# A decoder layer's recurrence: triangular products with a head's 64 columns as weights, two heads side by side, and turned back

## The chip, the cores and the metric

The kernel runs on one core of one Trainium2 chip. The metric is the device time of one execution in microseconds (us). Three executions of the kernel before took 2217.72 to 2218.32 us, median 2218.01 us.

## The reference, cut to what matters

The kernel computes one decoder layer on 256 tokens of width 2048, in float32: a SwiGLU feed-forward block, a mixer (sliding-window attention beside an RWKV-7 recurrence), cross-attention into a fixed memory, a second feed-forward block and a final norm. The parts that the change touches are the recurrence and the scores of the cross-attention:

```python
def rwkv7_scan(r, w, k, v, a, b):          # 16 heads of 64
    def step(S, inp):
        r_t, w_t, k_t, v_t, a_t, b_t = inp
        sa = jnp.einsum('bhij,bhj->bhi', S, a_t)
        S = S * w_t[:, :, None, :] + sa[..., None] * b_t[:, :, None, :] + v_t[..., None] * k_t[:, :, None, :]
        return S, jnp.einsum('bhij,bhj->bhi', S, r_t)
...
    s = jnp.einsum('bthd,bmhd->bhtm', q, km).astype(jnp.float32) * (CROSS_HEAD_DIM ** -0.5)
```

## The kernel before, in words

Precision first. A float32 product of the large matrices is done as three products of a faster format ("fp32r"): each operand is split into a high part, rounded by a ScalarE copy (line 345), and a low part, the rest, by a VectorE subtraction (line 346). Lines 438 to 440 multiply high by high, high by low and low by high into the same bank of PSUM. These are the main matrix products; their weights stream in through the SP queue in items of 1 MB or less. The recurrence and the cross-attention's scores use plain fp32 matmuls, which the profile records twice each.

The order of the work is written out by hand as an interleaving. Each background step is a Python generator; `bg.tick()` lets the first steps of each group (`const`, `feat`, `attn`, `ew`, `inverse`, `chain`, `norm`, `mem`) advance by one `yield`, and a tick comes after each six main matmuls or so. `yield from idle(n)` waits n ticks. A scheduler then orders each engine's queue: among instructions that its model finds ready, the one written first goes first. So a step's place in the trace is not its place in the file, and a `yield` moves a priority more than a time. `issue_after` adds an order on an engine's own queue.

The recurrence is solved in two chunks (c = 0, 1) of 128 tokens for two halves (h = 0, 1) of eight heads each. In `chain(h)` a half goes through these steps. `masked(c, m)` makes, per head, a 128 by 128 product of keys and receptances and masks it to a triangle (`mk`). `known(c)` multiplies `mk[c, 0]` by the values and, for c = 1, adds the state `s0` times the removal keys; the result is `u`. `solved(c)` multiplies the inverse of a triangle (`xb`) by `u`, giving `sa`. `results(c)` adds up three products into the output `yq`. Between the chunks the state `s0` is formed. `known` (line 1453) and `solved` (line 1470) use the triangle as the weights, 128 rows by 128 columns, and a head's 64 columns as the moving operand. `results` (line 1488) has it the other way round already: a head's 64 columns are the weights, the triangle moves, and the two heads of a pair write PSUM partitions 0 to 63 and 64 to 127 in turn. `invert(h)` builds `xb`, `finish(h)` normalises `yq` and leaves `yr`, the input of the products with `w_proj_rwkv`.

SBUF tiles come from pools with few buffers: `half` (five, for `u`, `sa`, `s0` and the like) and `t4` (20 of 4 KB per partition, for nearly all else in the mixer). PSUM has four single banks (`acc`) and two pairs (`two`); `acc` is shared by main products and chain steps.

Other places that the change touches: `late_vectors` (line 264) loads three small tables on the POOL queue; `to_features` (line 913) turns a product's tokens into features, one ScalarE copy out of PSUM; `attend` (line 924) is the windowed attention with its softmax on VectorE and ScalarE; `decay_and_rate` (line 1084), `substitute` (line 1235) and `invert` (line 1327) run ahead of the chain; `look_up` (line 1684) is the cross-attention, whose scores are fp32 matmuls at line 1693.

Of the kernel before, what the change touches and what calls it, by code (L numbers as in the profile page):

```python
# [142 lines left out]
def decoder_layer(ctx: ExitStack, tc: tile.TileContext, a: dict, out: bass.AP):  # L143
# [120 lines left out]
    def late_vectors():  # L264
        yield from idle(60)
        pool.dma_start(gains[:], a["g_later"])
        pool.dma_start(rv[:], a["v_rwkv"])
        pool.dma_start(sinks[:], a["attn_sinks"].broadcast_to([P, 16]))
        yield from idle(20)
        dve.tensor_scalar(nk_k[:], k_k, -1.0, None, ALU.mult)  # L270
        dve.tensor_scalar(ok_a[:], k_a, -1.0, 1.0, ALU.mult, ALU.add)
# [620 lines left out]
    with tc.tile_pool(name="mx", bufs=1, reuse_waits="tile") as sp:  # L892
# [20 lines left out]
        def to_features(tok, dst, name):  # L913
            last = act.copy(dst[:], feats(tok))
# [9 lines left out]
        def attend(kvs, qb):  # L924
# [32 lines left out]

            m, nm, es, den = (each(name) for name in ("m", "nm", "es", "den"))
            b3 = b[:].rearrange("p e (c w) -> p (e c) w", w=w)
            s3 = s[:].rearrange("p e c w -> p (e c) w")  # L960
# [21 lines left out]
            )  # L982
            yield from idle(5 if nk == 2 and kvs[0] else 4)
            pt = t4("pt", (P, 2, 4, P))
# [99 lines left out]
        def decay_and_rate():  # L1084
# [8 lines left out]
            for h in range(2):  # L1093
                cs.append(t4("cs"))
                aa.append(t4("aa"))
                for q in (0, 2):
                    b = two()
                    by_turns(
                        (
                            b[:, e, i * T : (i + 1) * T],  # L1100
                            wa[64 * e : 64 * e + 64, (4 * h + q + i) * P : (4 * h + q + i + 1) * P],
                            xwa[64 * e : 64 * e + 64, :],
                        )
                        for i in range(2) for e in (1, 0)
                    )
                    for i in range(2):
                        for e, (dst, bias) in enumerate(((cs[h], w0), (aa[h], a0))):
                            c = 4 * h + q + i
                            rates = act.activation(
                                dst[:, q + i, :], b[:, e, i * T : (i + 1) * T], AF.Sigmoid,  # L1110
                                bias=bias[:, c : c + 1],
                            )
                yield from idle(4)
            for h in range(2):
# [120 lines left out]
        def substitute():  # L1235
# [18 lines left out]
            pool.dma_start(xd[:].rearrange("i h u t -> (i h) u t"), xt[:])  # L1254
            act.copy(tmp[:96], xt[:96].rearrange("p u t -> p t u"))
            pool.dma_start(xe[:].rearrange("i h t u -> (i h) t u"), tmp[:96])
# [70 lines left out]
        def invert(h):  # L1327
# [60 lines left out]
            act.copy(n2_[low].rearrange("p c n t -> p c (n t)"), b[low])  # L1388
            yield
            b = two()  # L1390
# [19 lines left out]
        def chain(h):  # L1410
# [5 lines left out]
            ah, bh, kh, rh = at_[h], bt[h], aa[h], rt[h]  # L1416
            mk, u, sa = {}, {}, {}

# [16 lines left out]
            def masked(c, m):  # L1435
# [11 lines left out]
                )  # L1447

            def known(c):
                b = acc()  # L1450
                for j in range(4):
                    for e in range(2):
                        pe.matmul(  # L1453
                            b[:, of(j, e)], mk[c, 0][:, e, j, :], vtok[h][:, c, of(j, e)],
                            start=j + e == 0, stop=c == 0, **ek,
                        )
                if c:
                    for j in range(4):
                        pe.matmul(
                            b[:, at(j)], ah[:, j, at(c)], s0[:, at(j)], start=False, stop=True,  # L1460
                            **ek,
                        )
                u[c] = wide("u")
                act.copy(u[c][:], b)

            def solved(c):
                b = acc()
                for j in range(4):
                    for e in range(2):
                        pe.matmul(  # L1470
                            b[:, of(j, e)], xb[h][c][:, 4 * e + j, :], u[c][:, of(j, e)],
                            start=j + e == 0, stop=True, **ek,
                        )
                sa[c] = wide("sa")
                act.copy(sa[c][:], b)

# [31 lines left out]
            masked(0, 2)  # L1508
            yield
            solved(0)  # L1510
            bk = turned()
            masked(1, 0)
            yield
            results(0)
# [12 lines left out]
            masked(1, 2)  # L1527
            yield
            solved(1)
            yield  # L1530
            results(1)
# [142 lines left out]

        km, vm, qc = t4("km"), t4("vm", (P, 2, 512)), t4("qc")
        bg.until(lambda: hasattr(nm_, "r"))
# [7 lines left out]
        def look_up(t):  # L1684
# [7 lines left out]
            for h in range(4):  # L1692
                pe.matmul(b4[:, h], qc[:, h, ts], km[:, h, :], start=True, stop=True)
            dve.tensor_reduce(m[:], b4, AX.X, ALU.max)
# [160 lines left out]
```

## Time and profile before

| what | value |
|---|---|
| median of three executions | 2218.01 us |
| the profiled execution, its own time | 2218.37 us |
| its span, first to last instruction | 2216.6 us |
| TensorE (PE) busy | 2202.8 us |
| VectorE (DVE) busy | 1761.8 us |
| ScalarE (ACT) busy | 1197.5 us |

The profile has one row per instruction. PE is the matmul, PEld the weight load that runs beside it. A row `acc<-vtok,mk 128*128 128x64` is a matmul into a bank `acc`, from the tiles `vtok` and `mk`, with weights of 128 rows by 128 columns and a moving operand of 128 partitions by 64 columns. The view called the chain follows the work that ended last back to the start; there each row gives a start in us and the time by which the piece moved the end on, and xN is the number of records. A row of the timeline gives a start, a duration and, in brackets, the engine's idle time just before it and what ended that. Matmuls overlap, so a matmul's duration there is longer than its share of the engine's time.

### The profile page before, as it was taken

What the parts mean: (1) busy time and instruction counts of PE and PEld (TensorE: products, weight loads), DVE (VectorE), ACT (ScalarE), POOL (GpSimd) and SP (SyncE); (2) the same over time, 40 slices, a digit from 0 to 9 for tenths busy, and PEclk for the clock granted to TensorE, in tenths of its full rate; (3) what the DMA queues carried; (4) which work ended last, traced back from release to release, by engine and by line L of the source; (5) the groups of instructions that cost most, each with busy time, mean ns of one, the idle gap of its engine ahead of it and who ended that gap; (6) DMA issues with size and microseconds to landing.
All of it is one profiled execution on the core that took longest, in us unless ns stands there. A gap on an engine that the chain in (4) does not pass through costs nothing.

```text
span 2216.6 us, 28327 instructions
## 1 busy us (share of the span) xinstructions
PE 2202.8 (99%) x10774; PEld 1816.7 (82%) x10774; DVE 1761.8 (79%) x2053; ACT 1197.5 (54%) x1447; POOL 72.2 (3%) x141
## 2 busy tenths in 40 slices
PE   9999999999999999999999999999999999999998
PEld 7888888888888877888888888888888888888886
DVE  8988988898887477888556676558888988898887
ACT  6555555555555557534445455556555555555554
POOL 1000000000000000010400000000000000000000
PEclk9999999999999999999999999999999999999999
DMA  7665665565656545677714765557565565565564
GB/s 261 205 219 194 204 207 192 190 209 190 209 178 220 171 128 155 214 230 222 206 54 150 235 218 202 184 171 262 193 206 185 196 209 191 188 209 196 203 207 153
DMA packets 220536, 433.31 MB, mean 195 GB/s; under 512 B 13952, under 2 KB 16336, under 8 KB 220400
## 3 DMA queue, kind: packets, MB, share of 16 engines
q1 hardware_dynamic: 213200, 410.70, 56.0%
q0 software_dynamic: 6624, 20.14, 2.9%
q8 instruction: 84, 1.38, 0.2%
q10 hardware_dynamic: 576, 0.66, 0.1%
q14 instruction: 52, 0.43, 0.1%
HBM read 419.00 MB, written 12.45 MB: 195 GB/s over the span
## 4 chain that ended last, share of the span: by engine, by line
PE 96%; DVE 1%; DMA 1%; ACT 1%; issue 1%; SPq 0%; POOLq 0%; POOL 0%; ACTq 0%; DVEq 0%
PE acc L438 21%; PE acc L439 21%; PE acc L440 21%; PE two L438 9%; PE two L439 9%; PE two L440 9%; PE two L187 2%; PE two L179 1%; DMA raw<-in_ffn_w_up_dram 1%; DVE lo L346 1%; PE two L1351 0%; PE acc L1488 0%; PE acc L1453 0%; PE acc L1470 0%; PE acc L1351 0%
## 5 line engine op out<-in xcount | busy, mean ns | idle before, releaser
L345 ACT CAST hi<-raw 128x1024 fp32r<-128x1024 f32 (+1 forms) x769 | 762.8, 1001 | 791.8 <-PE two L440 370.5
L346 DVE TENSOR_TENSOR lo<-raw,hi 128x1024 fp32r<-128x1024 f32 (+1 forms) x770 | 884.3, 1158 | 321.2 <-ACT hi L345 320.0
L438 PE MATMUL acc<-hi,xhi 128*128 128x512 f32 (+1 forms) x1224 | 478.1, 391 | 1.2 <-ACT hi L345 0.8
L439 PE MATMUL acc<-lo,xhi 128*128 128x512 f32 (+1 forms) x1224 | 475.2, 388 | 1.3 <-DVE lo L346 1.3
L440 PE MATMUL acc<-hi,xlo 128*128 128x512 f32 (+1 forms) x1224 | 474.3, 388 | 0.0
L438 PEld LDWEIGHTS acc<-hi,xhi 128*128 128x128 f32 x1224 | 229.7, 188 | 52.9 <-issue 3.9
L439 PEld LDWEIGHTS acc<-lo,xhi 128*128 128x128 f32 x1224 | 230.0, 188 | 49.5 <-DVE lo L346 3.7
L440 PEld LDWEIGHTS acc<-hi,xlo 128*128 128x128 f32 x1224 | 229.9, 188 | 46.4 <-DVE xlo L712 0.2
L371 DVE TENSOR_TENSOR tlo<-raw,thi 128x1024 fp32r<-128x1024 f32 x160 | 193.1, 1221 | 0.0
L370 ACT CAST thi<-raw 128x1024 fp32r<-128x1024 f32 x160 | 165.7, 1050 | 33.3 <-DVE raw L365 18.8
L439 PE MATMUL acc<-lo,hhi 128*128 128x512 f32 x424 | 166.5, 393 | 0.0
L440 PE MATMUL acc<-hi,hlo 128*128 128x512 f32 x424 | 165.3, 390 | 0.0
L438 PE MATMUL acc<-hi,hhi 128*128 128x512 f32 x424 | 160.0, 391 | 0.1
L438 PE MATMUL two<-hi,xhi 128*128 128x512 f32 x352 | 138.5, 393 | 0.0
L439 PE MATMUL two<-lo,xhi 128*128 128x512 f32 x352 | 137.3, 390 | 0.0
L440 PE MATMUL two<-hi,xlo 128*128 128x512 f32 x352 | 137.2, 390 | 0.0
L365 DVE TENSOR_TENSOR raw<-raw 128x1024 f32<-128x1024 f32 x80 | 97.6, 1220 | 13.7 <-DMA raw<-in_ffn_w_up_dram 13.1
L439 PEld LDWEIGHTS acc<-lo,hhi 128*128 128x128 f32 x424 | 79.6, 188 | 19.0 <-DVE lo L346 2.9
L438 PEld LDWEIGHTS acc<-hi,hhi 128*128 128x128 f32 x424 | 79.2, 188 | 18.8 <-ACT hi L345 2.6
L440 PEld LDWEIGHTS acc<-hi,hlo 128*128 128x128 f32 x424 | 79.6, 188 | 16.2
L438 PEld LDWEIGHTS two<-hi,xhi 128*128 128x128 f32 x352 | 66.1, 188 | 14.7 <-DVE u L590 0.2
L440 PEld LDWEIGHTS two<-hi,xlo 128*128 128x128 f32 x352 | 66.1, 188 | 13.8
(403 smaller groups left out, 3199.0 us busy)
## 6 DMA issues: line engine op xcount, KB each, us to landing
raw<-in_ffn_w_gate_dram SPq DMA_DIRECT2D x171, 512.0 KB, 3.7
raw<-in_ffn_w_up_dram SPq DMA_DIRECT2D x167, 512.0 KB, 4.6
raw<-in_ffn_w_down_dram SPq DMA_DIRECT2D x152, 512.0 KB, 4.6
raw<-in_w_in_dram SPq DMA_DIRECT2D x136, 512.0 KB, 3.5
raw<-in_w_out_dram SPq DMA_DIRECT2D x32, 512.0 KB, 3.6
raw<-in_ffn_w_down_dram SPq DMA_DIRECT2D x12, 1024.0 KB, 5.0
raw<-in_w_proj_attn_dram SPq DMA_DIRECT2D x16, 512.0 KB, 3.5
raw<-in_w_proj_rwkv_dram SPq DMA_DIRECT2D x16, 512.0 KB, 4.3
```

The source lines that it names most:

```text
L179: prev = pe.matmul(to, lhs, rhs, **how)
L187: prev = pe.transpose(to, src, ident[:])
L345: newest["act"] = act.copy(hi[:, s], raw[:, s])
L346: newest["dve"] = dve.tensor_tensor(lo[:, s], raw[:, s], f32(hi[:, s]), ALU.subtract)
L365: dve.tensor_tensor(ta[:], raw[:, 1:3], raw[:, 0:2], ALU.subtract)
L370: act.copy(hi[:, s], t[:])
L371: dve.tensor_tensor(lo[:, s], t[:], f32(hi[:, s]), ALU.subtract)
L438: pe.matmul(o, xh, hi, start=first, stop=False, **how)
L439: pe.matmul(o, xh, lo, start=False, stop=False, **how)
L440: newest["pe"] = pe.matmul(o, xl, hi, start=False, stop=last, **how)
```

## The change

In `known` and `solved` the two operands change places: a head's 64 columns become the weights and the triangle moves. The two heads of a pair then write their 64 rows of PSUM beside each other, as `results` does. The output is turned round by that, so each result is copied to SBUF (`sideways`), turned back by four 128 by 128 transposes and copied out again (`turn_over`), in a tick of its own; the chain gets four more ticks per half. In `known(1)` the state's part is now multiplied first.

Six smaller edits come with it. The three small loads of `late_vectors` get a ScalarE write of one column each, placed behind the newest weight copy at that tick, so they can't start before. The cross-attention's `km` and `qc` are kept as high and low parts, and its scores become three fp32r products per head instead of one in fp32. `attend` waits two ticks more ahead of its first one-head softmax and one or two more ahead of the turned probabilities of the last heads. `decay_and_rate` waits seven ticks instead of four after each half. The ScalarE copy in `substitute` is cut in two, and `invert(0)` waits one tick more.

```diff
     def late_vectors():
         yield from idle(60)
+        with tc.issue_after(newest["act"].ins):
+            for v in (gains, rv, sinks):
+                act.activation(v[:, :1], g_ffn1[:, :1], AF.Copy)
         pool.dma_start(gains[:], a["g_later"])
...
         def to_features(tok, dst, name):
-            last = act.copy(dst[:], feats(tok))
+            src = feats(tok)
+            if isinstance(dst, list):
+                act.copy(dst[0][:], src)
+                dve.tensor_tensor(dst[1][:], src, f32(dst[0][:]), ALU.subtract)
+            else:
+                last = act.copy(dst[:], src)
...
+            if qb and not kvs[0]:
+                yield from idle(2)
...
-            yield from idle(5 if nk == 2 and kvs[0] else 4)
+            yield from idle(6 if kvs[0] > 1 else 4)
...
-                yield from idle(4)
+                yield from idle(7)
...
-            act.copy(tmp[:96], xt[:96].rearrange("p u t -> p t u"))
+            for t in (slice(0, 16), slice(16, 32)):
+                act.copy(tmp[:96, t], xt[:96, :, t].rearrange("p u t -> p t u"))
+                yield
...
-            yield
+            yield from idle(2 - h)
...
+            def turn_over(name):
+                b = acc()
+                turn((b[:, at(j)], side[0][:, at(j)]) for j in range(4))
+                t = wide(name)
+                act.copy(t[:], b)
+                return t
+
+            def sideways(b):
+                side[0] = wide("side")
+                act.copy(side[0][:], b)
+
             def known(c):
                 b = acc()
+                if c:
+                    for j in range(4):
+                        pe.matmul(
+                            b[:, at(j)], s0[:, at(j)], ah[:, j, at(c)], start=j == 0,
+                            stop=False, **ek,
+                        )
                 for j in range(4):
                     for e in range(2):
                         pe.matmul(
-                            b[:, of(j, e)], mk[c, 0][:, e, j, :], vtok[h][:, c, of(j, e)],
-                            start=j + e == 0, stop=c == 0, **ek,
+                            b[rows[e], at(j)], vtok[h][:, c, of(j, e)], mk[c, 0][:, e, j, :],
+                            start=c == 0 and j == 0, stop=True, **ek,
                         )
-                if c:
-                    for j in range(4):
-                        pe.matmul(
-                            b[:, at(j)], ah[:, j, at(c)], s0[:, at(j)], start=False, stop=True,
-                            **ek,
-                        )
-                u[c] = wide("u")
-                act.copy(u[c][:], b)
+                sideways(b)
 
             def solved(c):
                 b = acc()
                 for j in range(4):
                     for e in range(2):
                         pe.matmul(
-                            b[:, of(j, e)], xb[h][c][:, 4 * e + j, :], u[c][:, of(j, e)],
-                            start=j + e == 0, stop=True, **ek,
+                            b[rows[e], at(j)], u[c][:, of(j, e)], xb[h][c][:, 4 * e + j, :],
+                            start=j == 0, stop=True, **ek,
                         )
-                sa[c] = wide("sa")
-                act.copy(sa[c][:], b)
+                sideways(b)
...
             known(0)
             masked(0, 2)
             yield
+            u[0] = turn_over("u")
+            yield
             solved(0)
             bk = turned()
             masked(1, 0)
+            yield
+            sa[0] = turn_over("sa")
             yield
             results(0)
...
             known(1)
             masked(1, 2)
             yield
+            u[1] = turn_over("u")
+            yield
             solved(1)
+            yield
+            sa[1] = turn_over("sa")
             yield
             results(1)
...
-                pe.matmul(b4[:, h], qc[:, h, ts], km[:, h, :], start=True, stop=True)
+                for i, j in ((0, 0), (0, 1), (1, 0)):
+                    pe.matmul(
+                        b4[:, h], qc[i][:, h, ts], km[j][:, h, :],
+                        start=h % 2 + i + j == 0, stop=i == 1, skip_group_check=True,
+                    )
```

More of the change, by code (lines that the diff above doesn't have):

```diff
@@ L1416, in chain @@
             ah, bh, kh, rh = at_[h], bt[h], aa[h], rt[h]
-            mk, u, sa = {}, {}, {}
+            mk, u, sa, side = {}, {}, {}, {}
             def at(j):
@@ L1672, in decoder_layer @@
                 bg.spawn("mem", memory())
-        km, vm, qc = t4("km"), t4("vm", (P, 2, 512)), t4("qc")
+        km, qc = ([t4(n, dt=F32R) for _ in range(2)] for n in ("km", "qc"))
+        vm = t4("vm", (P, 2, 512))
         bg.until(lambda: hasattr(nm_, "r"))
```

## The prediction, made before the change was run

> **What bounds the kernel.** I read the page first: the span, the busy times, the granted clock and the chain.
>
> ```profile
> span 2216.6 us, 28327 instructions
> PE 2202.8 (99%) x10774; PEld 1816.7 (82%) x10774; DVE 1761.8 (79%) x2053; ACT 1197.5 (54%) x1447; POOL 72.2 (3%) x141
> PEclk9999999999999999999999999999999999999999
> PE 96%; DVE 1%; DMA 1%; ACT 1%; issue 1%; SPq 0%; POOLq 0%; POOL 0%; ACTq 0%; DVEq 0%
> ```
>
> PE carries 96% of the chain at full clock. An edit is therefore worth what it takes off PE's own work, or off the few places where PE stands. Next the busy time by stretch: the start, the attention, the substitution ahead of the recurrence, the recurrence itself, the cross-attention.
>
> ```profile
> core 0: us, PE busy (x) PEld busy (x) DVE busy (x) ACT busy (x) POOL busy (x), PEclk, DMA share, GB/s
> 0.00:20.00 20.00, 17.53 (x74) 13.99 (x75) 11.85 (x20) 12.29 (x21) 6.77 (x32) 1.00 0.92 320
> 760.00:860.00 100.00, 98.28 (x566) 77.04 (x565) 69.51 (x106) 63.97 (x118) 1.32 (x4) 1.00 0.44 131
> 950.00:1084.00 134.00, 134.00 (x615) 111.07 (x614) 102.51 (x135) 62.41 (x63) 27.91 (x46) 1.00 0.76 224
> 1084.00:1196.00 112.00, 111.56 (x1199) 95.10 (x1198) 64.76 (x70) 48.17 (x66) 12.85 (x24) 1.00 0.33 100
> 1446.00:1482.00 36.00, 35.94 (x172) 29.67 (x171) 18.38 (x26) 21.11 (x38) 0.00 (x0) 1.00 0.45 157
> ```
>
> PE stands 2.47 us in the first 20 us, 1.72 us in the attention, nothing in the substitution and 0.44 us in the recurrence. So the recurrence can gain only if its matmuls get cheaper, and waits can give back a few us at most. All of them together are below 5 us.
>
> **The swapped products.** The chain view of the recurrence's second half shows what each block adds to PE. L1453 is `known`, L1470 `solved`, L1488 `results`, L1499 the transposes of `turned`, L1518 the state, L1459 and L1481 products with the state, L438 and L439 main matmuls. A `known` or `solved` of eight fp32 matmuls is 16 records; a `results` is 32.
>
> ```profile
> 1162.22 1.94 PE acc L1453 x16
> 1166.84 1.73 PE acc L1470 x16
> 1168.57 0.90 PE two L1499 x8
> 1173.19 1.90 PE acc L1488 x32
> 1175.09 1.98 PE acc L1518 x16
> 1179.76 1.73 PE acc L1453 x16
> 1181.49 0.95 PE acc L1459 x8
> 1185.10 1.73 PE acc L1470 x16
> 1186.83 0.29 PE acc L438
> 1188.27 0.89 PE acc L1481 x8
> 1191.06 0.43 PE acc L438
> 1191.49 0.23 PE acc L439
> ```
>
> A `results` is two groups of 16 records in just the form that `known` and `solved` are to take: 64 columns as weights, a 128 by 128 triangle moving, two heads in turn. The timeline shows its two groups and their neighbours.
>
> ```profile
> 1172.81 0.39 PE L440 MATMUL acc<-hi,xlo 128*128 128x512 f32 x1
> 1173.12 1.09 PE L1488 MATMUL acc<-mk,vtok 128*64 128x128 f32 x16
> 1174.05 1.04 PE L1488 MATMUL acc<-mk,sa 128*64 128x128 f32 x16
> 1175.02 0.49 PE L1518 MATMUL acc<-vtok,bk 128*128 128x128 f32 x2
> ```
>
> From start to start a group is 0.93 to 0.97 us, so 0.95 us, where `known` and `solved` take 1.73. But the form has edges. It starts 0.31 us after a main matmul, against 0.23 between main ones: 0.08 to enter. The main matmul behind it moves the end by 0.43 instead of 0.23: 0.20 to leave, where the wide form leaves with 0.29: 0.06. Into wide fp32 work it leaves with 1.98 - 16 x 0.95/8 = 0.08 (L1518 against L1459's 0.95 for eight). Per half:
>
> - `known(0)`: 1.94 becomes 0.95 + 0.08 = 1.03; it goes into `masked` either way. Gain 0.91.
> - `known(1)`: 1.73 + 0.95 becomes 0.89 (the state's part first, as L1481 after main) + 0.95 + 0.08 = 1.92. Gain 0.76.
> - `solved(0)`: 1.73 becomes 1.03 + 0.08 into `turned`. Gain 0.62.
> - `solved(1)`: 1.73 becomes 1.03 + 0.20 - 0.06 to leave. Gain 0.56.
>
> That is 2.85 per half, 5.7 us for both. Against this stand eight `turn_over` of four transposes: half of L1499's 0.90 is 0.45 us, eight are 3.6, and 0.2 us for going back to main work once more (the 0.20 above) in the first half, whose steps run closer together. Net gain of this part: 1.9 us. Bounds: with no edges at all 8 x (1.73 - 0.95) - 3.6 = 2.6 and 0.21 more for the first `known` of each half, about 3.0; with an edge of 0.20 at each turn-over, 1.9 - 1.6 = 0.3. I stay near the middle because `turned` and `results` are the same forms in the same place.
>
> The row of L1488 also decides whether two heads side by side run together at all: 0.93/16 = 0.058 us per record, where L1518's full-width records take 1.90/16 = 0.119. The Trainium skill ("TensorE: Matmul & The Clock Gate", Part 3, The mechanism) says that a weight load overlaps running matmuls only when the row group differs; two heads side by side share all rows. By that rule nothing would be saved and the sum would be the second rival's, 2.2 us slower; by the row it is 3.5 us faster. The row contradicts the rule here, so I go by the row.
>
> Each half has eight ScalarE copies of one bank here instead of four: eight more in all.
>
> ```profile
> 1182.47 0.59 ACT L1464 COPY u<-acc 128x512 f32<-128x512 f32 x1 [1.63 <-PE acc L1459]
> L1470 PE MATMUL acc<-u,xb 128*128 128x64 f32 x64 | 7.8, 275 | 0.0
> ```
>
> At 0.59 us they are 4.7 us on an engine that is busy 48 of 112 us: no bound. The wait is what counts: a turn-over waits for the side copy, the product behind it for the turned copy. A tick's six main matmuls are 6 x 0.23 = 1.4 us of cover, against 0.59, or 0.59 behind a 1.05 us cast. Today's same wait, `solved` behind the copy of `u`, costs PE 0.0 us. I take 0; the price without cover is a rival. The eight further ticks and the delays in `attend`, `decay_and_rate`, `substitute` and `invert` move the end of `finish(1)` by 17 ticks at most (six in `decay_and_rate`, some four in `attend`, three in `substitute` and `invert`, four in the last chain), 17 x 1.4 = 24 us. There is room:
>
> ```profile
> L668 ACT CAST yr<-yq x4: 612/620/622, 1202.6 to 1232.5; 128x512 fp32r<-128x512 f32 x4
> L438 PE MATMUL acc<-hi,yr x64: 388/390/479, 1264.0 to 1309.5; 128*128 128x512 f32 x64
> ```
>
> The last `yr` is copied at 1232.5 and the first matmul on it starts at 1264.0: 31 us. So these delays cost nothing; were that cover gone, each tick beyond it would cost its 1.4 us. And the halved copy in `substitute` gains nothing either, since PE never stood there (134.00 of 134.00). POOL's queue behind the later copy has only loads for `invert`, inside the same 31 us.
>
> **Scores of the cross-attention.** 16 records (eight fp32 matmuls, 256 columns) become 24 fp32r matmuls of 256 columns, a form that L1593 has.
>
> ```profile
> 1199.46 1.90 PE two L1593 x16
> 1450.80 3.45 PE two L1693 x16
> PEld two L1693 <- ACT qc L914: 0.2, 1, 0.2
> L1057 DVE TENSOR_TENSOR d<-p 128x1024 f32<-128x1024 f32 x6 | 7.4, 1226 | 4.5 <-ACT p L1054 4.5
> ```
>
> 24 x 1.90/16 = 2.85: 0.6 us less. But today's matmuls already wait 0.2 us for the copy of `qc`, and now the third of them needs `qc`'s low part, a VectorE subtraction of the shape at 1.23 us that begins after that copy. If PE stands for it, the part loses 0.6; if main matmuls go in between, as they do elsewhere, it gains 0.6. I take a gain of 0.5, since the low part is wanted only by the third matmul and main work is at hand.
>
> **Start and attention.**
>
> ```profile
> v_rwkv<-in_v_rwkv_dram POOLq DMA_DIRECT2D x1, 41.5 KB, 5.3
> g_later<-in_g_later_dram POOLq DMA_DIRECT2D x1, 32.0 KB, 5.6
> 16.40 2.00 ACT L345 CAST hi<-raw 128x1024 fp32r<-128x1024 f32 x2 [0.84 <-DMA raw<-in_ffn_w_up_dram]
> 18.76 0.19 PEld L439 LDWEIGHTS acc<-lo,xhi 128*128 128x128 f32 x1 [0.60 <-DVE lo L346]
> 777.83 0.50 PE L439 MATMUL acc<-lo,xhi 128*128 128x512 f32 x1 [0.60 <-DVE lo L346]
> PE two L187 <- DVE s L980: 0.6, 1, 0.6
> ```
>
> The first 20 us run the DMA engines at 0.92 and 320 GB/s. Without the two larger tables' 73.5 KB there the weights behind them land at least 73.5/320 = 0.23 us earlier, and at most the 0.60 us that the weights' wait at 18.76 lasts can go: 0.4. The tables then load beside a feed-forward stretch that is not short of DMA, behind them on POOL's queue little waits, as POOL is busy 72 us in all; three one-column ScalarE writes cost nothing on ACT at 54%. In the attention the two waits of 0.60 and 0.6 us come from softmaxes that crowd VectorE; the added ticks pull them apart. They may open another wait of that size, so 0.7 of the 1.2 (bounds: gain 1.2, loss 0.6).
>
> **Sum.** 1.9 + 0.5 + 0.4 + 0.7 = 3.5 us. The profiled execution took 2218.37 us (span 2216.6 and 1.8 around it) and becomes 2214.9; it lies 0.36 above the median, so against 2218.01 I forecast 2214.5 us. The parts' ends add up to a gain of 3.0 + 0.6 + 0.6 + 1.2 = 5.4 and to a loss of 0.7 (0.3 - 0.6 + 0.23 - 0.6 = -0.67): 2212.6 to 2218.7. The forecast proper is what lies above 2213.6 in that.
>
> **Rivals.** Less than 0.2% (4.4 us) can't be told from no change for this kernel.
>
> *Deeper gain.* The ends above come together: few edges, both attention waits gone, the deferred loads worth their whole wait. 5.4 us: 2212.6. For it: 0.93 us for a group directly behind main work. Against: 0.43 behind L1488 is no accident of one place.
>
> *The swap doesn't pay.* Two heads side by side don't run together for `known` and `solved`. Then the eight groups cost what they do now (16 x 0.119 = 1.90), the turn-overs' 3.6 + 0.2 come on top, and the small edits give 1.6: 2.2 us slower than before, 2220.2. For it: nothing in the rows. Against it stands L1488, the same form.
>
> *Slower: the copies come out into the open.* The chain now has 16 copies that PE waits for directly, one before and one after each turn-over. If the scheduler puts no main matmul between, each shows its 0.59 us: 16 x 0.59 = 9.4 on top, 2223.9. It decides from (2222.4 - 2214.5)/16 = 0.5 us per copy on, so nearly all must show. For it: ACT has 1.05 us casts that a copy may queue behind. Against it: the 0.0 of L1470 today.
>
> **Chances.** Deeper gain 0.28; forecast 0.54; small losses at the score products and in the attention that eat the gain up, 0.07; a swap that doesn't pay 0.03; slower 0.08. The deeper gain, 1.0 us past the 4.4, counts as faster; the next three as the same. The range goes from 2211.0, a little past the deeper gain for a term I missed, to 2220.2; what lies outside is slower and some of the deep end, 0.14 together.
>
> **What would show it.** Right: L1453 and L1470 with 64-column weights, 16 records in about 1.0 us of the chain view; new transposes of `side`, four records in 0.45; L1693 with 24 records in 2.9; no wait at 18.76. Wrong: PE waits for ACT on `side` or `u` in the wait view, a low part of `qc` that holds L1693 for a us, waits of PE for VectorE in the attention beyond 0.6 us, or idle time ahead of the first matmul on `yr`.

## The result and the profile after

The changed kernel takes 2212.84 us (median of ten executions, 2212.00 to 2213.79), the kernel before 2217.99 us beside it (ten executions). The ratio is 0.9975 with a 95% interval of 0.9966 to 0.9983: 5.15 us or 0.25% faster. That is the place of the rival called *deeper gain* (2212.6 us), not of the forecast (2214.5 us). The profiled execution took 2212.88 us.

The page of the changed kernel, span, TensorE (PE) busy and the chain's shares:

```profile
span 2210.8 us, 28427 instructions
PE 2198.5 (99%) x10814; PEld 1810.5 (82%) x10814; DVE 1764.9 (80%) x2055; ACT 1203.1 (54%) x1459; POOL 71.6 (3%) x141
PE 98%; DMA 0%; ACT 0%; DVE 0%; issue 0%; POOLq 0%; POOL 0%; SPq 0%; ACTq 0%; DVEq 0%
```

Of the 5.8 us by which the span shrank, PE's own busy time gives 4.3 (2202.8 to 2198.5), waits give the rest. Busy time by stretch, the same five stretches as before:

```profile
core 0: us, PE busy (x) PEld busy (x) DVE busy (x) ACT busy (x) POOL busy (x), PEclk, DMA share, GB/s
0.00:20.00 20.00, 17.31 (x74) 14.15 (x75) 12.44 (x21) 12.54 (x22) 5.03 (x29) 1.00 0.92 334
760.00:860.00 100.00, 99.53 (x574) 78.15 (x573) 68.97 (x104) 62.46 (x112) 1.33 (x4) 1.00 0.47 140
1084.00:1196.00 112.00, 111.83 (x1205) 93.20 (x1204) 58.23 (x62) 48.03 (x66) 26.86 (x45) 1.00 0.42 119
```

The attention's standstill falls from 1.72 to 0.47 us; the start gains nothing (2.47 us of idle time before, 2.69 now). In the recurrence PE stands 0.17 us where it stood 0.44, so nearly all that this stretch gains is cheaper work. The chain view shows that work. In this kernel L1482 is `known`, L1476 the part of the state that `known(1)` multiplies first, L1492 `solved`, L187 with a bank `acc` the transposes of `turn_over`, L441 to L443 the main matmuls:

```profile
1131.24 1.09 PE acc L1482 x16
1153.48 1.09 PE acc L1476 x8
1154.57 1.02 PE acc L1482 x16
1160.28 0.59 PE acc L187 x4
1166.45 1.02 PE acc L1492 x16
1169.06 0.44 PE acc L187 x4
1173.68 0.87 PE acc L1482 x16
1177.23 0.43 PE acc L187 x4
1179.06 1.02 PE acc L1492 x16
1182.20 0.43 PE acc L441
1183.79 0.44 PE acc L187 x4
```

A product of 16 records moves the end by 0.87 to 1.09 us, where it took 1.73 to 2.00. A turn-over is 0.43 to 0.59 us. Its copies cost PE almost nothing: the view of the tile `side` lists who waited for it, and PE's weight load did once, for 0.2 us. What it lost to the copies into `u` and `sa` lies within the 0.17 us for which it stands in the whole window.

```profile
L1470 ACT COPY side<-acc x8: 567/586/587, 1132.4 to 1201.2; 128x512 f32<-128x512 f32 x8
  PEld acc L187: 0.2, 1
```

To see where the 5.8 us of the span went, I cut both profiled executions at the starts of main matmuls on certain inputs. The stretches are: the start up to the last product on `hhi` in the first feed-forward; from there to the first on `yahi`, which holds the attention; from the last on `ya` to the first on `yr`, which holds the recurrence; from the first on `mehi` to the first on `ochi`, which holds the cross-attention's scores. The table gives, for this kernel and for every experiment below, how much longer or shorter than in the kernel before each stretch is (us), and the ratio of the times with its interval, where there were enough executions for one.

| kernel | start | attention | recurrence | scores | ratio to the kernel before |
|---|---|---|---|---|---|
| changed | +0.19 | -1.82 | -3.23 | -0.45 | 0.9975 (0.9966 to 0.9983) |
| e1, the chain's swap alone | +0.53 | +0.01 | -2.69 | 0.00 | 0.9988 (0.9980 to 0.9997) |
| e2, the small edits alone | +0.41 | -1.81 | -0.49 | -0.46 | 0.9987 (0.9978 to 0.9996) |
| e3, the two delays of `attend` alone | +1.54 | -1.87 | +0.67 | -0.01 | 0.9997 (0.9988 to 1.0006) |
| e4, changed, heads one after the other | -0.17 | -1.83 | +0.69 | -0.45 | 0.9991 (0.9981 to 1.0000) |
| e5, changed, without the added steps | -0.47 | -1.82 | -2.71 | -0.47 | 0.9978 (0.9969 to 0.9987) |
| e6, changed, tables loaded at the start | -0.21 | -1.82 | -3.25 | -0.45 | 0.9974 (0.9963 to 0.9985) |
| e7, changed, without the delays ahead of the chain | -0.24 | -1.83 | -2.05 | -0.45 | 0.9977 (0.9968 to 0.9987) |
| e8, changed, scores by part | -0.09 | -1.82 | -3.25 | -0.58 | 0.9971 (0.9960 to 0.9982) |
| e9, changed, whole copy in `substitute` | -0.07 | -1.83 | -3.79 | -0.45 | one execution |
| e10, changed, without the first delay of `attend` | -0.26 | -1.53 | -3.25 | -0.45 | one execution |
| e11, changed, without the second | -0.51 | -1.01 | -3.77 | -0.46 | one execution |
| e12, e8 and e9 together | +0.34 | -1.83 | -3.79 | -0.59 | 0.9969 (0.9957 to 0.9981) |

Attention, recurrence and scores repeat to 0.1 us from kernel to kernel where nothing in them was changed (the recurrence of e11 apart, which is told below). So they tell apart what the times, with intervals of some 2 us to each side, cannot. The start does not repeat: it scatters over 2 us. One more stretch differs, from the first product of the second feed-forward on `chi` to its first on `hhi`: 0.59 us shorter in the changed kernel. It is 0.54 shorter in e1 and 0.43 in e2, which share no edit, and 0.54 longer in e3, so I count it to no edit. What moved it stays open.

### The profile page after: what moved, and what is told of

Same layout as the page of the kernel before. It is cut to its first block, busy times and chain, and to the rows that moved or that the text cites. A ratio compares the mean times of both kernels' runs of the same rounds, so it can differ in the third digit from the quotient of the medians.

```text
span 2210.8 us, 28427 instructions
## 1 busy us (share of the span) xinstructions
PE 2198.5 (99%) x10814; PEld 1810.5 (82%) x10814; DVE 1764.9 (80%) x2055; ACT 1203.1 (54%) x1459; POOL 71.6 (3%) x141
## 4 chain that ended last, share of the span: by engine, by line
PE 98%; DMA 0%; ACT 0%; DVE 0%; issue 0%; POOLq 0%; POOL 0%; SPq 0%; ACTq 0%; DVEq 0%
PE acc L441 21%; PE acc L442 21%; PE acc L443 21%; PE two L442 9%; PE two L441 9%; PE two L443 9%; PE two L187 2%; PE two L179 1%; PE two L1363 0%; PE acc L1509 0%; DMA raw<-in_ffn_w_up_dram 0%; PE acc L179 0%; PE acc L1363 0%; PE two L1164 0%; PE acc L1492 0%
## 5 line engine op out<-in xcount | busy, mean ns | idle before, releaser
L441 PE MATMUL acc<-hi,xhi 128*128 128x512 f32 (+1 forms) x1224 | 478.3, 392 | 1.5 <-ACT xhi L714 0.8
L443 PE MATMUL acc<-hi,xlo 128*128 128x512 f32 (+1 forms) x1224 | 473.8, 387 | 0.0
L441 PEld LDWEIGHTS acc<-hi,xhi 128*128 128x128 f32 x1224 | 229.6, 188 | 54.0 <-issue 4.3
L443 PEld LDWEIGHTS acc<-hi,xlo 128*128 128x128 f32 x1224 | 229.8, 188 | 46.6 <-DVE xlo L715 0.2
L443 PE MATMUL acc<-hi,hlo 128*128 128x512 f32 x424 | 165.1, 389 | 0.0
L441 PE MATMUL acc<-hi,hhi 128*128 128x512 f32 x424 | 159.9, 391 | 0.0
L441 PE MATMUL two<-hi,xhi 128*128 128x512 f32 x352 | 138.3, 393 | 0.0
L443 PE MATMUL two<-hi,xlo 128*128 128x512 f32 x352 | 137.0, 389 | 0.0
L441 PEld LDWEIGHTS acc<-hi,hhi 128*128 128x128 f32 x424 | 79.1, 188 | 18.8 <-ACT hi L348 2.6
L443 PEld LDWEIGHTS acc<-hi,hlo 128*128 128x128 f32 x424 | 79.6, 188 | 16.2
L441 PEld LDWEIGHTS two<-hi,xhi 128*128 128x128 f32 x352 | 66.1, 188 | 14.7 <-DVE u L593 0.2
L443 PEld LDWEIGHTS two<-hi,xlo 128*128 128x128 f32 x352 | 66.1, 188 | 13.9
```

Of the source, the lines that this page charges most:

```text
L441: pe.matmul(o, xh, hi, start=first, stop=False, **how)
L443: newest["pe"] = pe.matmul(o, xl, hi, start=False, stop=last, **how)
```

## Experiments

The first question was which of the parts gave the gain, and whether two heads side by side are what makes the products cheap. Four kernels answer it.

**e1 and e2: the two halves of the change.** e1 is the kernel before with only the edits of `chain` (`known`, `solved`, `turn_over`, `sideways` and the four steps per half). e2 is the changed kernel with the old `chain`.

```diff
+            def sideways(b):
+                side[0] = wide("side")
+                act.copy(side[0][:], b)
...
-                            b[:, of(j, e)], xb[h][c][:, 4 * e + j, :], u[c][:, of(j, e)],
-                            start=j + e == 0, stop=True, **ek,
+                            b[rows[e], at(j)], u[c][:, of(j, e)], xb[h][c][:, 4 * e + j, :],
+                            start=j == 0, stop=True, **ek,
```

> Only the swap in the recurrence with its turn-overs and their ticks, on the kernel before. Theory: the swap is worth 3.2 us of PE's work, all of it between the first matmul on yahi and the first on yr, so the median falls by 3 to 3.5 us and no other stage moves by more than 0.2 us. Rival: the 3.2 us need the shifted ticks of the small edits too (fewer changes between forms on PE); then the swap alone gives the 1.9 us that the prediction's edges allow, or less.

> All the small edits without the swap. Theory: they are worth the other part: 1.8 us in the attention, 0.45 us in the cross-attention's scores, 0.6 us at the head of the second feed-forward block and 0 at the start, together 2.5 us. Rival: the gain at the second feed-forward block belongs to the swap; then 2.0 us.

Measured: 2216.37 and 2215.71 us beside 2218.79 us of the kernel before, ratios 0.9988 and 0.9987. By stretch the recurrence is 2.69 us shorter with the swap alone and 0.49 with the small edits alone; together they make 3.18 of the 3.23 in the changed kernel. The attention and the scores belong to e2 alone. So the halves add up, and neither carries the change by itself.

The trace of e1 also says of what the 2.69 us are made. I summed the times from the start of one PE record to the next, by the kinds of the two records, between the last product on `ya` and the first on `yr`. Inside the groups of `known` and `solved` (120 pairs) 13.37 us become 6.57: 6.80 less. Inside the turn-overs (24 pairs) 2.72 us are new. What is left, -2.69 + 6.80 - 2.72 = 1.39 us, is all else. Most of it is edges, the changes between one form and another, of which the eight new blocks of transposes bring more. The expectation had 3.2 us or, by the rival, 1.9 or less; 2.69 lies between them.

**e3: the two delays of `attend` alone,** in the kernel before.

```diff
+            if qb and not kvs[0]:
+                yield from idle(2)
...
-            yield from idle(5 if nk == 2 and kvs[0] else 4)
+            yield from idle(6 if kvs[0] > 1 else 4)
```

> Only the two edits of ticks in attend. Theory: they alone pull the softmaxes apart and give the attention's 1.8 us, with both waits of 0.6 us gone. Rival: the seven ticks in decay_and_rate, which follow on the attention, give part of it; then about 1.2 us, the two visible waits.

Measured: 2217.94 us, ratio 0.9997 (0.9988 to 1.0006), no difference that can be told. But the attention is 1.87 us shorter, as in the changed kernel and as the expectation had it for these two delays alone. Against that the recurrence stretch lost 0.67 us and the second feed-forward 0.54. (The start that was 1.54 us longer belongs to the profiled execution, at 2219.66 us the slowest of the ten; it says nothing of the median.) Inside the recurrence stretch the wait view of e3 shows a wait that the kernel before does not have:

```profile
PE two L187 <- ACT tok L907: 1.3, 1, 1.3
```

This became a question of its own; e7 and e9 take it up.

**e4: heads one after the other.** The changed kernel with all products of one head of each pair ahead of those of the other, in `known` and `solved`; the same matmuls, in another order.

```diff
-                for j in range(4):
-                    for e in range(2):
+                for e in range(2):
+                    for j in range(4):
```

> The changed kernel, with the loops over heads and pairs exchanged in known and solved: all four first heads of the pairs, then all four second heads, so neighbours no longer write different halves of PSUM. Theory: the gain comes from two heads running side by side; then a record costs about 0.11 us again instead of 0.055, the eight groups are 1.75 us each, and the kernel is 8 x 0.8 = 6.4 us slower than the changed one, 1 us slower than before. Rival: the gain comes from the shorter weight load of 64 columns alone; then the groups stay at 0.95 us and the time at that of the changed kernel.

Measured: 2216.70 us, ratio 0.9991 (0.9981 to 1.0000), and a recurrence 3.92 us longer than in the changed kernel (+0.69 against -3.23). The chain view of e4:

```profile
1155.21 1.51 PE acc L1482 x16
1161.41 0.59 PE acc L187 x4
1167.57 1.51 PE acc L1492 x16
1175.29 1.36 PE acc L1482 x16
1181.16 1.51 PE acc L1492 x16
```

A group of 16 takes 1.36 to 1.58 us here against 0.87 to 1.09. From start to start within `solved`, a record takes 54.8 ns in the changed kernel, 87.3 ns here and 111.3 ns in the kernel before (60 pairs each). With 120 such pairs in `known` and `solved`, 120 x (87.3 - 54.8) ns = 3.9 us: just the loss. So the gain needs two heads side by side. That the narrow weights alone don't give it was expected; that part of it stays with the heads apart was not. The last section shows that this part too comes from two heads running at once.

The next question was the rival in which the copies come out into the open.

**e5: without the added steps.** Each turn-over is in the same step as its product.

```diff
             known(0)
             masked(0, 2)
-            yield
             u[0] = turn_over("u")
...
             solved(1)
-            yield
             sa[1] = turn_over("sa")
```

> The changed kernel without the four added steps of each half: each turn_over now stands right behind its product, and nothing can be issued between the product, the copy of `side` and the transposes. The theory that the copies are hidden by main matmuls of a step: PE now waits for ScalarE at each of the eight transposes of `side`, for the copy of 0.58 us and the way there and back, some 0.6 to 0.8 us each, and the stretch from the last `ya` to the first `yr` grows by 8 x 0.7 = 5.6 us less four steps a half that end earlier (not on the path); about 4.5 to 6 us slower than the changed kernel, so all of its gain is gone. The rival, that PE's order or the planner finds other work anyway: no wait, within 1 us of the changed kernel.

Measured: 2213.98 us, ratio 0.9978 (0.9969 to 0.9987), recurrence 0.52 us longer than in the changed kernel. No 5 us came. The expectation overlooked that `masked` and `turned` stand between most products and their `turn_over`, and behind `solved(1)`, where nothing does, it took the order in the file for the order on PE. The chain view of e5 shows what stands between a product and its transposes:

```profile
1152.10 1.02 PE acc L1492 x16
1153.13 0.42 PE acc L441
1154.26 0.44 PE acc L187 x4
...
1173.52 1.02 PE acc L1482 x16
1174.54 1.09 PE two L179 x16
1175.63 0.59 PE acc L187 x4
1177.62 1.02 PE acc L1492 x16
1178.64 1.02 PE two L1520 x8
1179.66 1.09 PE two L179 x16
1180.75 0.59 PE acc L187 x4
```

Behind `known` comes a `masked` of 1.09 us, behind `solved(0)` come `turned` and a `masked`, together 2.11 us, each longer than the copy of 0.59 us. Where the step holds no such block (`solved(1)`, the first three rows), the order that the scheduler writes puts main matmuls there. So the copies are hidden twice over, and the rival is further off than the prediction had it: the added steps are not needed to hide them. They are worth 0.5 us.

**e6: the tables loaded at the start again.**

```diff
-        with tc.issue_after(newest["act"].ins):
-            for v in (gains, rv, sinks):
-                act.activation(v[:, :1], g_ffn1[:, :1], AF.Copy)
```

> The changed kernel with the three late tables loaded at the start again. If the deferral is worth the 0.4 us of the prediction, the anchor at the end of the first feed-forward's hi/thi products (52.96 us) is 0.4 us later, and the time 0.4 us longer. If it is worth nothing, as the two traces suggest (both reach 52.96 us), the wait of 0.6 us at about 18.8 us is back and that anchor stays within the 0.5 us that the start scatters by; later stages stay where they are: attention -1.8 us, recurrence -3.2 us against the kernel before.

Measured: 2213.16 us, ratio 0.9974 (0.9963 to 0.9985); every later stretch is the changed kernel's, and the start is not longer. The wait at 18.8 us did not come back either, against my expectation. In the kernel before, the weight loads of L439 waited twice for `lo` in the first 55 us, 1.3 us in all. In e6, with the tables at the start, there is one such wait left, as in the changed kernel:

```profile
PEld acc L439 <- DVE lo L346: 0.7, 1, 0.7
```

But e6 is one execution. Over all fourteen traces the wait at 18.8 to 19.8 us is there in three of the four kernels that load the tables at the start (the kernel before, e1 and e3, not e6) and in none of the ten that defer them. So the tables may well have a hand in it; e6 shows only that the wait can fail to come with them early. Nor is its length what PE loses. PE's own row in the kernel before shows that the matmul behind that weight load stood for 0.18 us:

```profile
18.76 0.50 PE L439 MATMUL acc<-lo,xhi 128*128 128x512 f32 x1 [0.18 <-DVE lo L346]
```

In e3 it was 0.62 us. By the table the start of the four kernels with early tables is on average 0.5 us longer than that of the kernel before, which is one of them, and that of the ten others 0.1 us shorter. But the four alone scatter over 1.75 us, and the times of e6 show no loss. A worth of some tenths of a us for the deferral is neither shown nor excluded.

**e7 and e9: the delays ahead of the chain, and the copy in `substitute`.** e7 takes out the delays in `decay_and_rate` and `invert` and makes the copy whole; e9 only makes the copy whole, by which the two ticks between and behind its halves go too.

```diff
-                yield from idle(7)
+                yield from idle(4)
...
-            for t in (slice(0, 16), slice(16, 32)):
-                act.copy(tmp[:96, t], xt[:96, :, t].rearrange("p u t -> p t u"))
-                yield
+            act.copy(tmp[:96], xt[:96].rearrange("p u t -> p t u"))
...
-            yield from idle(2 - h)
+            yield
```

> The changed kernel without the delays in decay_and_rate and invert and with the copy in substitute whole again. If those delays account for the 0.5 us that the kernel with the small edits alone gained in the recurrence, the stretch from the last `ya` to the first `yr` gains 2.7 us against the kernel before instead of 3.2, and the time is 0.5 us above the changed kernel's. If that 0.5 us came from elsewhere (or the delays cost nothing, as predicted), the stretch still gains 3.2 us.

> The changed kernel with the ScalarE copy in substitute whole again, the delays kept. Without the delays too, TensorE waited 1.2 us for `tok`, whose copies stood behind that copy of 2.13 us on ScalarE. If the delays cure this, the copies of `tok` stay ahead of the whole copy, there is no wait, and the stretch from the last `ya` to the first `yr` keeps its gain of 3.2 us against the kernel before. If halving the copy is what cures it, the wait of some 1.2 us comes back and the stretch gains 2.0 us.

Measured: e7 2213.77 us, ratio 0.9977 (0.9968 to 0.9987), recurrence -2.05, which is neither of the values expected; e9 2211.85 us in one execution, recurrence -3.79. The timeline of ScalarE in e7 shows the cause, and the wait view what PE lost:

```profile
1031.53 2.13 ACT L1265 COPY tmp<-xt 96x1024 f32<-96x1024 f32 x1 [0.89 <-DVE xt L1262]
1033.57 1.25 ACT L910 ACTIVATE tok<-acc,rs 128x512 f32<-128x512 f32 x2
```

```profile
PE two L187 <- ACT tok L910: 1.2, 1, 1.2
```

The copies of `tok` stand behind the copy of 2.13 us on ScalarE, and PE waits 1.2 us for `tok`. In the changed kernel the same place reads:

```profile
1031.57 0.69 ACT L910 ACTIVATE tok<-acc,rs 128x512 f32<-128x512 f32 x1 [0.30 <-PE acc L443]
1032.93 0.69 ACT L910 ACTIVATE tok<-acc,rs 128x512 f32<-128x512 f32 x1 [0.67 <-PE acc L443]
1038.12 2.26 ACT L1266 COPY tmp<-xt 96x512 f32<-96x512 f32 x2 [0.53 <-DVE xt L1262]
```

The delayed copy comes 5 us behind `tok`. In e9 it is whole, still late (1037.84), and nothing waits. So the delays cure the wait without the halves; whether the halves alone would cure it, no run shows. The wait itself is a child of `attend`: e1, with the old `attend` and no delays, doesn't have it; e3 and e7, with the new `attend` and no delays, have it with 1.3 and 1.2 us. The two sets of delays belong together: one gains 1.8 us in the attention, and without the other 1.2 of it is paid back 200 us later. Without that wait, e7's stretch would be some 3.3 us shorter than the kernel before's and e3's 0.6 (-2.05 and +0.67, less waits of 1.24 and 1.26). So the 0.5 us of the small edits comes with the shift in the attention and not with the delays; 0.2 of it is a wait of PE for `n` at 1111 us, which the kernel before and e1 have and e2, e3 and e7 don't.

That the whole copy leaves the recurrence 0.56 us shorter than the changed kernel's was not expected. It is no direct price of the two half copies, since e11 has the half copies and the same -3.77. Of the 0.56 us, 0.11 is a wait for `mk` at 1131 us that the changed kernel has and e9 and e11 don't. The matmuls are the same, and the sums over pairs of records differ mainly in which forms follow one another. An order of the work a little later or earlier falls out better or worse by half a us here; what decides it I could not settle.

**e10 and e11: which delay of `attend` does what.** The changed kernel, without the first (two ticks ahead of the one-head softmax) and without the second (ahead of the turned probabilities).

```diff
-            if qb and not kvs[0]:
-                yield from idle(2)
```

```diff
-            yield from idle(6 if kvs[0] > 1 else 4)
+            yield from idle(5 if nk == 2 and kvs[0] else 4)
```

> The changed kernel without the two ticks ahead of the first one-head softmax in attend. The changed kernel gains 1.8 us between the end of the first feed-forward and the first `yahi`. If the first delay carries the 0.60 us wait for `lo` at about 778 us and the work behind it, that gain falls by 0.6 to 1.2 us and the wait is back; if the second delay does it all, it stays at 1.8 us.

> The changed kernel with the old delay ahead of the turned probabilities in attend. If the second delay carries the 0.6 us wait of the transposes for the softmax's `s`, the gain of 1.8 us between the end of the first feed-forward and the first `yahi` falls by 0.4 to 0.8 us and that wait grows from 0.2 to 0.6 us; if the first delay does it all, it stays at 1.8 us.

Measured: the attention's gain falls from 1.82 to 1.53 us without the first, to 1.01 without the second. Each brings its own wait back; the wait views of e10 and then of e11 between 716 and 920 us:

```profile
PE acc L442 <- DVE lo L349: 0.6, 1, 0.6
```

```profile
PE two L187 <- DVE s L990: 0.8, 2, 0.6
```

In the changed kernel the first wait is absent and `s` is waited for once, for 0.2 us, at 779 us. The 0.8 us of e11 are that wait and one of 0.6 us at 817.5. So the first delay removes a wait of 0.6 us and is worth 0.3, the second removes another of 0.6 us and is worth 0.8. In the attention PE stands 0.83 us in e11 and 0.47 in the changed kernel, so some 0.4 us of the second's worth are PE's own work. The timelines show where it may come from. In the kernel before, a block of eight products of the probabilities `pt` with `vt` is split in two around six transposes:

```profile
822.51 0.65 PE L179 MATMUL acc<-pt,vt 128*64 128x256 f32 x2
823.09 0.88 PE L187 MATMUL two<-ident,tok 128*128 128x128 f32 x6
823.89 1.08 PE L179 MATMUL acc<-pt,vt 128*64 128x256 f32 x6
```

In the changed kernel that block is whole:

```profile
825.36 1.08 PE L179 MATMUL acc<-pt,vt 128*64 128x256 f32 x8
```

The records of these products start in pairs, too, 7 ns apart. In the split block the first two records start 266 ns apart and the last two 217. e11 has the same split, e3 and e10 don't.

**e8: the scores by part.**

```diff
-            for h in range(4):
-                for i, j in ((0, 0), (0, 1), (1, 0)):
+            for i, j in ((0, 0), (0, 1), (1, 0)):
+                for h in range(4):
```

> The changed kernel with the score products ordered by part first (four high by high, four with the low part of `km`, then four with the low part of `qc`) instead of by head. The third matmul no longer needs the low part of `qc`, which is wanted from the ninth on, 1 us later. If the 0.3 us wait of TensorE for VectorE at the scores is on the path, it goes, and the stretch from the first `mehi` to the first `ochi` gains 0.75 us against the kernel before instead of 0.45. If main work or another copy fills that time anyway, it stays at 0.45. A loss of up to 0.3 us if the change between heads costs more than the change of parts. In the time, at most 0.3 us, which the rounds can't tell.

Measured: 2212.62 us, ratio 0.9971 (0.9960 to 0.9982), the scores' stretch 0.13 us shorter than in the changed kernel. The rows of the changed kernel's chain, and its wait for the low part of `qc`:

```profile
1446.10 0.24 PE two L1724 x2
1447.27 2.73 PE two L1724 x22
```

```profile
PEld two L1724 <- DVE qc L920: 0.3, 1, 0.3
```

In the changed kernel main work stands after the second product, ahead of the first that needs the low part. In e8 there is no such wait row, and main work stands after the eighth product, as its chain shows:

```profile
1445.79 0.96 PE two L1724 x8
1446.97 1.98 PE two L1724 x16
```

The wait's 0.3 us was a weight load's, mostly hidden; less than half of it was on the path.

**e12: a version meant to beat both.** The whole copy of e9 and the order of e8.

> A version meant to beat both kernels: the changed kernel with the copy in substitute whole and the score products ordered by part. Each alone left the stretch it touches shorter than the changed kernel's: 0.56 us between the last `ya` and the first `yr`, 0.13 us between the first `mehi` and the first `ochi`. If these add up, the two stretches gain 3.8 and 0.58 us against the kernel before, and the time lies some 0.7 us below the changed kernel's, near 2212.1 us or 0.9969 of the kernel before. If the 0.56 us hangs on an order that the other edit shifts, the first stretch falls back to a gain of 3.2 us.

Measured: 2212.13 us, ratio 0.9969 (0.9957 to 0.9981); recurrence -3.79 and scores -0.59, as expected. It is faster than the kernel before by 6.9 us. That it beats the changed kernel is shown by the two stretches (0.56 and 0.14 us), not by the times, whose intervals overlap.

## Why the prediction was right or wrong

**The swapped products: right, and the size of the edges too large.** The prediction gave each group 0.95 us and 0.08 for its edge; the chain shows 0.87 to 1.09. It gave a turn-over 0.45; the chain shows 0.43 to 0.59. The sum of 1.9 us came out as 2.7 (e1), inside its bounds of 0.3 to 3.0. What was mis-sized are the edges. Against the 6.80 - 2.72 = 4.08 us that the inside of the groups gained, a net of 1.9 left 2.2 us for all else, edges above all; the trace has 1.39. Part of the 0.8 us between them may be luck, since the same matmuls in another order made 0.56 us in this stretch (e9).

**Two heads side by side: right.** The rival in which they don't run together needed a record of 0.119 us; it is 0.055. The Trainium skill ("TensorE: Matmul & The Clock Gate", Part 3, The mechanism) lets a weight load overlap running matmuls only when the row group differs. These pairs share all rows, and e4 shows that the order of the two column halves alone is worth 3.9 us; so the measurement decides against the rule as the prediction applied it. The Trainium skill ("TensorEngine Tiling (Array Packing)", When to Use Tiling) lists swapping the operands with two-fold column tiling for a moving side of up to 64 columns. The trace agrees with the factor of two: 111.3 to 54.8 ns is 2.03 times; after turning back and edges, 2.7 us of the 6.8 are left.

**The copies: right that they cost nothing.** The reason given, main matmuls of an added step, was only half of it. By e5 the copies stay hidden without the steps, behind `masked` and `turned` and behind main matmuls that the scheduler moves in. The point at which that rival decides, 0.5 us per copy, is far off.

**The delays and the halved copy: the cost was right, the use was missed.** The 17 ticks were predicted to fit into 31 us of room ahead of the first product on `yr`. They do. Both starts, the last copy's and the first matmul's:

```profile
L671 ACT CAST yr<-yq x4: 598/617/623, 1218.1 to 1247.1; 128x512 fp32r<-128x512 f32 x4
L441 PE MATMUL acc<-hi,yr x64: 389/389/476, 1259.3 to 1304.8; 128*128 128x512 f32 x64
```

There are still 12 us between them. But the step that these delays cost nothing, and that the halved copy gains nothing since PE never stood there, looked only at the kernel before. PE does stand there once the attention has shifted, and the delays are what prevents it: 1.2 us (e7). That the halved copy gains nothing was right (e9). The 0.5 us by which the small edits shorten the recurrence by themselves (e2) was in no term.

**The scores: right.** Predicted 0.5, measured 0.45, and 0.45 to 0.47 in every experiment with this edit but the two that reorder it.

**The attention: right in kind, too small.** Predicted 0.7 with a bound of 1.2; measured 1.8. The bound was the sum of the two waits. These did go, but PE stands 0.47 us in the attention now where it stood 1.72, so waits give 1.25 of the 1.8 us. A third wait, 0.44 us for `tok` at 852 us, was in the 1.72 of the prediction's own table and not in its bound; with the other two gone, waits of 0.23 and 0.24 us are what is left. The other 0.57 us are PE's own work. By the sums over pairs of records with the idle time taken out, 0.42 of them lie inside the products of `pt` with `vt` (42 pairs, 4.65 to 4.23 us), where the split block is whole now; the changes from one form to another cost as much as before (13.8 and 13.9 us). The step that failed took two waits for all that an edit of the order can move.

**The start: not shown, and its bound misread.** The 0.4 us for the deferred tables can't be seen in e6, whose start is no longer than the changed kernel's. The wait of 0.60 us at 18.76 us, read as the tables' doing, is absent there, but it is present in the three other kernels with early tables and in none of the ten without. The step that failed took that 0.60 us for what PE can win. It is the row of a weight load; PE itself stood 0.18 us there. Whether the deferral is worth any of it stays open.

**The sum.** By the stretches it is 2.7 + 0.5 in the recurrence, 1.8 in the attention and 0.45 for the scores, 5.5 us, less 0.2 in the stretch between the attention and the recurrence, where the 3.5 forecast were 1.9, 0.7, 0.5 and a start of 0.4. The *deeper gain* had the right size (5.4), in part by luck. Of its three conditions the few edges came true only in part (2.7 of 3.0), the tables gave nothing that can be seen, and the attention gave more than its two waits. What made up for the missing start, 0.6 us in the attention and 0.5 in the recurrence, was in no term. The 0.59 us in the second feed-forward, which belongs to no edit, was not in any either.

## What to carry to other kernels

Where a group of fp32 products with 64 moving columns is on TensorE's path, compare it with the swapped form of the same kernel, two heads in turn on the two halves of the columns; here a record fell from 111 to 55 ns, and turning back cost four transposes and two copies that other work hid. Judge a delay together with the stretch after it: a shift that removes one wait moved another copy ahead of a needed one, and only a second delay kept the gain. And before a wait of half a us at the start is charged to a cause, or the cause dismissed, count in how many executions with the cause and without it the wait is there; and read its price from the matmul's row, not from the weight load's.

## What was unexpected on the hardware

In the changed kernel the starts of the 16 records of a `solved` alternate, some 7 ns and 102 to 104 ns apart, behind a first pair that takes 160: the records start in pairs, and a pair takes about what one wide record took (111 ns). With the heads apart (e4) most gaps are 109 ns at both ends of a group, but in its middle seven gaps together are 384 ns, 55 ns each. In all eight groups the starts can be read as two series of eight records, each 109 ns from record to record behind a first gap of 160 (but for one), of which the second begins 5 or 6 ns after the fifth record of the first. The trace doesn't name the head of a record, so that these series are the two heads is a reading. By it a record of one head alone takes 109 ns where a wide one took 111: the narrow weights by themselves give next to nothing, and the second head starts beside the first though the first head's records are all issued ahead. That is why e4 lost 3.9 us and not the 6.4 that its expectation gave for no overlap at all. How far ahead this can reach was not measured.
